# Half of the first norm's modulation tiles as the stationary operand of TensorE, and eleven tile buffers

## The chip, the core and the metric

One core of a Trainium2 chip runs the whole kernel. The metric is the device time of one execution in microseconds (us), as the median of three runs. Beside it stands one profiled execution, in which every instruction is recorded.

## The reference, cut to what matters

The program is a block with a state-space scan, a gating unit and a mixture of experts, followed by a two-layer attention block. The change touches only the first thing that it computes from its conditioning vectors, the shift and scale of the first norm:

```
mod_l = silu(c)     @ ada_w + ada_b      # c, c_ctx: 1024 values; ada_w: 1024 x 6144
mod_c = silu(c_ctx) @ ada_w + ada_b
sh1, sc1 = first two blocks of 1024 of mod_l (and of mod_c)
xm_c = rmsnorm(ctx, norm1_w) * (1 + sc1_c) + sh1_c     # 256 x 1024
xm_l = rmsnorm(x,   norm1_w) * (1 + sc1_l) + sh1_l     # 512 x 1024
```

All later work takes `xm_l` and `xm_c` as input. So two vectors (latent and context) are multiplied with the first 2048 columns of `ada_w`, which is a matrix of 1024 rows: 8 MB in float32.

## The kernel before, in words

`main` (L750) runs `setup`, loads parameters, and calls `norm_x` (L223), `ada01` (L176), `mod_x` (L252) and `scan` (L314). The kernel is written against a framework that records instructions, tracks their dependences and then writes a fixed order for each engine: earlier lines of the program have priority, and where an instruction isn't ready, a later one that is goes ahead of it. So the order on an engine is fixed at build time, and at run time each engine takes its own list in turn and waits where an input is not there.

`norm_x` loads six 128x1024 blocks of tokens (`xin`, L233), squares and sums them on ScalarE (L235), makes the inverse root on VectorE (`rsqrt`, L151), scales the blocks (L241) and turns them with 48 TensorE transposes of 128x128 into `aux` banks of PSUM (L248), from where ScalarE and VectorE copy them to `xr` (L249). There are four `aux` banks and four `mm` banks (L90, L93).

`ada01` makes the shift and scale. The 16 tiles `araw` are loaded by SyncE's queue in the order j = 0, 1 (the 1024 columns of shift, then of scale) and k = 0 to 7 (the 128-row blocks of `ada_w`); there are eight buffers for them (L202, L203). Float32 products are made of the engine's rounded float32 format by splitting an operand in a high and a low part. Each tile passes `split` (L101): ScalarE writes the high part `whi` (L106), VectorE the low part `wlo` (L107). The two vectors are split as well and stand as four columns `st[:, k]`, which are the stationary operand; the tile's parts move, 512 columns at a time. That is four matmuls for a tile (L207 twice, L208 twice), each with 4 stationary columns and 512 moving ones, summed over k in two `mm` banks of 4 rows. The result is copied by ScalarE to `ada_res` (L210). Then 16 small matmuls (L213, eight for each j) with `ada_res` as the stationary operand and a selection matrix `sel` of two columns as the moving one add high and low and turn rows to columns: 128 features on the partitions, two columns for each block, all in one `aux` bank `pm`. These are plain float32 matmuls, and each is issued as two pairs of a weight load and a matmul. VectorE makes `shf` and `scl` of them (L218 to L220).

`mod_x` applies them, with ScalarE (L265), VectorE (L266, L267) and GpSimd (L267), and what it writes is the input of `dt_proj` (L346) and of the projections (L272), whose products are L115 to L117.

SyncE's queue carries all loads. It has at most eight loads under way: load n waits until load n-8 has landed. In program order behind the tiles stand six loads of the scan: `dsk` (L325), `w_dt` (L98), `dtb` and `alog` (L364), and two weight tiles `w_xbc` (L98). As the ninth `araw` tile has to wait for a buffer, the order before puts these six between the eighth and the ninth tile.

Elsewhere the same form of matmul as in L213 is found in the router of the experts (L853): a whole float32 tile of 128x128 as the stationary operand and 16 moving columns.

```
201            for k in range(8):
202                raw = e1.tile([128, 1024], F32, name="araw", tag="araw", bufs=8)
203                nc.sync.dma_start(raw, self.a["ada"][k * 128:(k + 1) * 128, j * 1024:(j + 1) * 1024])
204                wh, wl = self.split(raw, 1024)
```

Of the kernel before, what the change touches and what calls it, by code (L numbers as in the profile page):

```python
# [8 lines left out]
F32 = mybir.dt.float32  # L9
# [28 lines left out]
class Net:  # L38
# [51 lines left out]
    def mm(self):  # L90
        return self.ps.tile([128, 512], F32, name="mm", tag="mm", bufs=4)
# [84 lines left out]
    def ada01(self):  # L176

        nc, sm = self.nc, self.c1
        ct = sm.tile([128, 16], F32, name="ct")
        th = sm.tile([128, 16], F32, name="cth")  # L180
        nc.scalar.activation(th, self.PA[:, 0:16], AF.Tanh, scale=0.5)
        nc.vector.tensor_scalar(ct, self.PA[:, 0:16], 0.5, None, op0=OP.mult)
        self.cs = cs = self.c1.tile([128, 16], F32, name="cs")
        nc.vector.scalar_tensor_tensor(cs, th, 1.0, ct, op0=OP.add, op1=OP.mult)
        st = self.c1.tile([128, 8, 4], F32R, name="cst")
        nc.vector.tensor_copy(st[:, :, 0], cs[:, 0:8])
        nc.vector.tensor_copy(st[:, :, 2], cs[:, 8:16])
        nc.vector.tensor_tensor(st[:, :, 1], cs[:, 0:8], st[:, :, 0].bitcast(F32), OP.subtract)
        nc.vector.tensor_tensor(st[:, :, 3], cs[:, 8:16], st[:, :, 2].bitcast(F32), OP.subtract)
        jp = sm.tile([4, 2], I32, name="jp4")  # L190
        nc.gpsimd.iota(jp, pattern=[[-2, 2]], base=0, channel_multiplier=1)
        s1 = sm.tile([4, 2], F32, name="s1")
        sel = sm.tile([4, 2], F32, name="sel")
        nc.vector.tensor_scalar(s1, jp, 0.0, None, op0=OP.is_ge)
        nc.vector.tensor_scalar(sel, jp, 1.0, None, op0=OP.is_le)
        nc.vector.tensor_tensor(sel, sel, s1, OP.mult)
        e1 = self.e1
        res = e1.tile([4, 2048], F32, name="ada_res")
        for j in range(2):
            pp = [self.mm(), self.mm()]  # L200
            for k in range(8):
                raw = e1.tile([128, 1024], F32, name="araw", tag="araw", bufs=8)  # L202
                nc.sync.dma_start(raw, self.a["ada"][k * 128:(k + 1) * 128, j * 1024:(j + 1) * 1024])  # L203
                wh, wl = self.split(raw, 1024)
                for q in range(2):
                    c = slice(q * 512, (q + 1) * 512)
                    nc.tensor.matmul(pp[q][:4], st[:, k], wh[:, c], start=k == 0, stop=False)  # L207
                    nc.tensor.matmul(pp[q][:4], st[:, k], wl[:, c], start=False, stop=k == 7)  # L208
            for q in range(2):
                nc.scalar.copy(res[:, j * 1024 + q * 512:j * 1024 + (q + 1) * 512], pp[q][:4])  # L210
        pm = self.aux()
        for b in range(16):
            nc.tensor.matmul(pm[:, 2 * b:2 * b + 2], res[:, b * 128:(b + 1) * 128], sel, start=True, stop=True)  # L213
        pv = pm[:, :32].rearrange("p (b s) -> p s b", s=2)
        self.scl = self.c1.tile([128, 2, 8], F32, name="scl")
        self.shf = self.c1.tile([128, 2, 8], F32, name="shf")
        for s in range(2):
            nc.vector.tensor_tensor(self.shf[:, s], pv[:, s, 0:8], self.PA[:, 24:32], OP.add)  # L218
            nc.vector.scalar_tensor_tensor(self.scl[:, s], pv[:, s, 8:16], 1.0, self.PA[:, 32:40], op0=OP.add, op1=OP.add)
            nc.vector.tensor_tensor(self.scl[:, s], self.scl[:, s], self.PA[:, 16:24], OP.mult)  # L220
        e1.release()
# [1844 lines left out]
```

## Time and profile before

| What | Value |
|---|---|
| Median of 3 runs | 3218.07 us (3213.55 to 3218.97) |
| Profiled execution, its own time | 3218.56 us |
| Its span | 3216.8 us (1.76 us of its time lie around the span) |
| TensorE busy (matmul) | 3053.1 us, 95% |
| VectorE, ScalarE, GpSimd busy | 70%, 50%, 12% |
| Mean granted clock of TensorE | 0.977 of full speed |
| First instruction of `mod_x` | 47.16 us after the span's start |

The profile gives busy time for each engine, a record for each instruction with its start and duration, what ended the idle time ahead of it, and the clock that TensorE was granted. A matmul's end is modelled, so the pace of a row of matmuls is read from their starts. PE stands for TensorE's matmuls, PEld for its weight loads, DVE for VectorE, ACT for ScalarE, POOL for GpSimd, SPq for SyncE's queue of loads.

### The profile page before, as it was taken

The numbers are of one execution on the slowest core, as the hardware profiler recorded it, in microseconds if no ns is written. First come the engines' busy times: TensorE is split into PE (matmuls) and PEld (weight loads), VectorE is DVE, ScalarE is ACT, GpSimd is POOL, SyncE is SP. The second block draws the span as 40 slices with busy tenths as digits, with TensorE's granted clock in tenths as the row PEclk, the third lists the DMA queues.
The fourth block names the chain that finished last, engine by engine and source line by source line (L and its number), as shares of the span: only waits on it lengthen the run. The fifth ranks groups of instructions, "written<-read, shape, count | busy, mean of one in ns | idle before, by whom it ended". The sixth has DMA issues, their size and how long they took to land. (4 is left out here: it accounts for less than half of the span.)

```text
span 3216.8 us, 43492 instructions
## 1 busy us (share of the span) xinstructions
PE 3053.1 (95%) x16242; PEld 2484.7 (77%) x16242; DVE 2255.6 (70%) x3786; ACT 1592.5 (50%) x2715; POOL 378.3 (12%) x295
## 2 busy tenths in 40 slices
PE   7999899969999999699999999999999999999998
PEld 4887677756656556578787789988888777799986
DVE  7778764468988878767575588863776655688844
ACT  6545432228767667356353435552464444445531
POOL 1454200032211111200011000000000010000000
PEclk9999999979999999899999999999999999999999
DMA  5112434549999997311215333332312224323322
GB/s 193 53 46 73 144 122 147 197 179 393 371 345 348 347 335 271 105 59 60 86 47 173 99 118 99 106 98 93 105 53 74 79 99 140 110 92 109 106 92 79
DMA packets 140781, 470.06 MB, mean 146 GB/s; under 512 B 16268, under 2 KB 20364, under 8 KB 140568
## 3 DMA queue, kind: packets, MB, share of 16 engines
q1 hardware_dynamic: 139416, 463.08, 41.4%
q0 software_dynamic: 1152, 4.19, 0.4%
q8 instruction: 127, 2.08, 0.3%
q14 instruction: 86, 0.70, 0.1%
HBM read 456.71 MB, written 10.50 MB: 145 GB/s over the span
## 5 line engine op out<-in xcount | busy, mean ns | idle before, releaser
L107 DVE TENSOR_TENSOR wlo<-raw,whi 128x1024 fp32r<-128x1024 f32 (+4 forms) x340 | 379.3, 1118 | 310.8 <-ACT whi L106 309.5
L106 ACT CAST whi<-raw 128x1024 fp32r<-128x1024 f32 (+4 forms) x340 | 317.7, 936 | 412.1 <-PE mm L116 155.4
L115 PE MATMUL mm<-xTh,whi 128*128 128x512 f32 (+2 forms) x880 | 344.1, 391 | 4.8 <-ACT P L1240 2.6
L116 PE MATMUL mm<-xTh,wlo 128*128 128x512 f32 (+3 forms) x880 | 340.7, 388 | 0.0
L117 PE MATMUL mm<-xTl,whi 128*128 128x512 f32 (+2 forms) x880 | 338.8, 386 | 1.1 <-DVE xTl L267 0.6
L115 PE MATMUL mm<-whi,xTh 128*128 128x512 f32 (+1 forms) x536 | 206.8, 388 | 6.1 <-DVE zt L562 3.5
L117 PE MATMUL mm<-wlo,xTh 128*128 128x512 f32 (+1 forms) x536 | 204.5, 387 | 3.8 <-DVE wlo L107 3.8
L116 PE MATMUL mm<-whi,xTl 128*128 128x512 f32 (+1 forms) x536 | 206.9, 386 | 0.0
L115 PEld LDWEIGHTS mm<-xTh,whi 128*128 128x128 f32 (+1 forms) x880 | 165.5, 188 | 45.5 <-ACT P L1240 4.2
L117 PEld LDWEIGHTS mm<-xTl,whi 128*128 128x128 f32 (+1 forms) x880 | 165.3, 188 | 38.1 <-DVE xTl L267 2.2
L116 PEld LDWEIGHTS mm<-xTh,wlo 128*128 128x128 f32 (+1 forms) x880 | 165.6, 188 | 34.3 <-issue 1.2
L1013 PE MATMUL mm<-wlo,XS 128*128 128x512 f32 x336 | 113.6, 412 | 15.7 <-DVE wlo L952 13.2
L115 PEld LDWEIGHTS mm<-whi,xTh 128*128 128x128 f32 x536 | 101.4, 189 | 27.5 <-DVE zt L562 4.3
L1404 POOL TENSOR_TENSOR ql<-q,qh 128x512 fp32r<-128x512 f32 x16 | 20.7, 1292 | 862.6 <-ACT qh L1403 862.6
L117 PEld LDWEIGHTS mm<-wlo,xTh 128*128 128x128 f32 x536 | 101.3, 189 | 23.6 <-DVE wlo L107 4.2
L116 PEld LDWEIGHTS mm<-whi,xTl 128*128 128x128 f32 x536 | 101.4, 189 | 19.5
L952 DVE TENSOR_TENSOR wlo<-mraw,whi 128x1024 fp32r<-128x1024 f32 x82 | 107.0, 1328 | 12.8 <-ACT whi L950 12.2
L1012 PE MATMUL mm<-whi,XS 128*128 128x512 f32 x336 | 111.5, 408 | 2.5 <-ACT whi L950 2.5
L950 ACT CAST whi<-mraw 128x1024 fp32r<-128x1024 f32 x96 | 97.6, 1048 | 26.3 <-PE mm L1012 22.9
L1240 ACT ACTIVATE P<-mm,smv 128x512 f32<-128x512 f32 x128 | 88.2, 691 | 31.7 <-DVE P L1528 16.0
L115 PE MATMUL mm<-whi,hh 128*128 128x512 f32 x248 | 94.9, 398 | 8.1 <-ACT hh L1854 8.0
L107 DVE TENSOR_TENSOR flo<-fs,fhi 128x1024 fp32r<-128x1024 f32 x80 | 97.7, 1221 | 5.7 <-ACT fhi L106 4.6
(827 smaller groups left out, 8664.2 us busy)
## 6 DMA issues: line engine op xcount, KB each, us to landing
raw<-w_f SPq DMA_DIRECT2D x92, 512.0 KB
raw<-w_gate SPq DMA_DIRECT2D x68, 512.0 KB
mraw<-w_gate SPq DMA_DIRECT2D x52, 512.0 KB
mraw<-w_down SPq DMA_DIRECT2D x49, 512.0 KB
araw<-ada SPq DMA_DIRECT2D x48, 512.0 KB
mraw<-w_up SPq DMA_DIRECT2D x43, 512.0 KB
rawu<-w_f SPq DMA_DIRECT2D x40, 512.0 KB
PT<-w_up SPq DMA_DIRECT2D x30, 512.0 KB
```

Source lines behind the costliest of these rows:

```text
L106: nc.scalar.copy(hi[:, :n], raw[:, :n])
L107: nc.vector.tensor_tensor(lo[:, :n], raw[:, :n], hi[:, :n].bitcast(F32), OP.subtract)
L115: mm(out, ah, bh, start=first, stop=False)
L116: mm(out, al, bh, start=False, stop=False)
L117: mm(out, ah, bl, start=False, stop=last)
L950: nc.scalar.copy(hi, raw)
L952: eng.tensor_tensor(lo, raw, hi.bitcast(F32), OP.subtract)
L1012: nc.tensor.matmul(pp[q], X[:, k], wh[:, c], start=k == 0, stop=False)
L1013: nc.tensor.matmul(pp[q], X[:, k], wl[:, c], start=False, stop=k == 7)
L1240: nc.scalar.activation(P, s, AF.Exp, bias=v[:, 8 + i:9 + i], accum_out=v[:, 16 + i:17 + i])
L1404: nc.gpsimd.tensor_tensor(ql, q, qh.bitcast(F32), OP.subtract)
```

## The change

Of the eight tiles of each j, four still pass `split` and the moving matmuls (k = 0, 2, 4, 6 for j = 0 and k = 0, 1, 3, 4 for j = 1). The other four are used as they land: each of their eight 128x128 blocks is the stationary operand of a plain float32 matmul with the two silu columns of that k as the moving operand. These sum directly in `pm`, where the L213 matmuls of the four split tiles are added too; `pm` is begun by the first whole-tile matmul and never cleared again. The eight L213 matmuls of each j follow the copies of that j. The tiles have eleven buffers in place of eight.

```
-        for j in range(2):
+        c2 = cs.rearrange("p (s k) -> p k s", s=2)
+        mm = nc.tensor.matmul
+        pm = self.aux()
+        out = lambda b: pm[:, 2 * b:2 * b + 2]
+        begun = False
+        for j, rows in enumerate(((0, 2, 4, 6), (0, 1, 3, 4))):
             pp = [self.mm(), self.mm()]
             for k in range(8):
-                raw = e1.tile([128, 1024], F32, name="araw", tag="araw", bufs=8)
+                raw = e1.tile([128, 1024], F32, name="araw", tag="araw", bufs=11)
                 nc.sync.dma_start(raw, self.a["ada"][k * 128:(k + 1) * 128, j * 1024:(j + 1) * 1024])
+                if k not in rows:
+                    for b in range(8):
+                        mm(out(8 * j + b), raw[:, b * 128:(b + 1) * 128], c2[:, k], start=not begun, stop=True, skip_group_check=begun)
+                        begun = True
+                    continue
                 wh, wl = self.split(raw, 1024)
                 for q in range(2):
                     c = slice(q * 512, (q + 1) * 512)
-                    nc.tensor.matmul(pp[q][:4], st[:, k], wh[:, c], start=k == 0, stop=False)
-                    nc.tensor.matmul(pp[q][:4], st[:, k], wl[:, c], start=False, stop=k == 7)
+                    mm(pp[q][:4], st[:, k], wh[:, c], start=k == rows[0], stop=False)
+                    mm(pp[q][:4], st[:, k], wl[:, c], start=False, stop=k == rows[-1])
             for q in range(2):
                 nc.scalar.copy(res[:, j * 1024 + q * 512:j * 1024 + (q + 1) * 512], pp[q][:4])
-        pm = self.aux()
-        for b in range(16):
-            nc.tensor.matmul(pm[:, 2 * b:2 * b + 2], res[:, b * 128:(b + 1) * 128], sel, start=True, stop=True)
+            for b in range(8 * j, 8 * j + 8):
+                mm(out(b), res[:, b * 128:(b + 1) * 128], sel, start=False, stop=True, skip_group_check=True)
```

## Rows read from the trace of the kernel before

**Rows 1.** The page: busy time of TensorE, and its busy tenths in 40 slices.
```profile
PE 3053.1 (95%) x16242; PEld 2484.7 (77%) x16242; DVE 2255.6 (70%) x3786; ACT 1592.5 (50%) x2715; POOL 378.3 (12%) x295
...
PE   7999899969999999699999999999999999999998
```
**Rows 2.** Timeline 39 to 48: start us, us, engine, line, operation, tiles, count [idle before].
```profile
39.71 1.05 ACT L106 CAST whi<-araw 128x1024 fp32r<-128x1024 f32 x1 [0.20 <-DMA araw<-ada]
...
42.30 0.62 PE L208 MATMUL mm<-wlo,cst 128*4 128x512 f32 x2
...
43.28 1.05 ACT L210 COPY ada_res<-mm 4x512 f32<-4x512 f32 x2
...
43.91 2.72 PE L213 MATMUL aux<-sel,ada_res 4*128 4x2 f32 x16 [0.99 <-ACT ada_res L210]
46.66 0.17 DVE L218 TENSOR_TENSOR shf<-aux,PA 128x8 f32<-128x8 f32 x1 [1.81 <-PE aux L213]
...
47.16 9.69 ACT L265 ACTIVATE xTh<-xr,shf,scl 128x512 fp32r<-128x512 f32 x16 [2.83 <-DVE scl L220]
```
**Rows 3.** Timeline of PE alone, 14 to 37.
```profile
14.43 1.01 PE L207 MATMUL mm<-whi,cst 128*4 128x512 f32 x2 [10.88 <-ACT whi L106]
...
16.68 1.05 PE L207 MATMUL mm<-whi,cst 128*4 128x512 f32 x2
17.54 1.05 PE L208 MATMUL mm<-wlo,cst 128*4 128x512 f32 x2
...
20.10 1.03 PE L207 MATMUL mm<-whi,cst 128*4 128x512 f32 x2
...
23.82 0.62 PE L208 MATMUL mm<-wlo,cst 128*4 128x512 f32 x2
24.27 0.63 PE L207 MATMUL mm<-whi,cst 128*4 128x512 f32 x2
...
27.76 1.31 PE L248 MATMUL aux<-ident,xin 128*128 128x128 f32 x10 [0.36 <-ACT xr L249]
28.82 0.70 PE L208 MATMUL mm<-wlo,cst 128*4 128x512 f32 x2
...
33.72 1.94 PE L213 MATMUL aux<-sel,ada_res 4*128 4x2 f32 x16
35.59 0.63 PE L208 MATMUL mm<-wlo,cst 128*4 128x512 f32 x2
36.06 0.62 PE L207 MATMUL mm<-whi,cst 128*4 128x512 f32 x2
```
**Rows 4.** One tile's instructions (araw): count, duration ns min/median/max, first and last start.
```profile
L106 ACT CAST whi<-araw x16: 1030/1046/1056, 13.3 to 39.7; 128x1024 fp32r<-128x1024 f32 x16
L107 DVE TENSOR_TENSOR wlo<-araw,whi x16: 1214/1219/1227, 14.6 to 41.0; 128x1024 fp32r<-128x1024 f32 x16
```
**Rows 5.** Timeline of SyncE's queue: the araw loads before and behind the other six.
```profile
4.56 7.82 SPq L203 DMA_DIRECT2D araw<-ada  x8
...
21.05 8.60 SPq L203 DMA_DIRECT2D araw<-ada  x8
```
**Rows 6.** Timeline of PE: the router's whole tiles as stationary operand, at either clock.
```profile
663.09 3.44 PE L853 MATMUL aux<-wrp,xT 128*128 128x16 f32 x16
...
683.19 1.85 PE L853 MATMUL aux<-wrp,xT 128*128 128x16 f32 x16
```
**Rows 7.** Windows: busy of PE, PEld, DVE, ACT, POOL (counts), granted clock, DMA share, GB/s.
```profile
662.69:666.10 3.41, 3.18 (x16) 3.21 (x17) 0.09 (x1) 0.93 (x4) 0.44 (x3) 0.50 0.37 154
...
683.17:686.58 3.41, 3.31 (x30) 3.19 (x28) 2.66 (x11) 1.71 (x7) 0.00 (x0) 1.00 1.00 390
686.58:689.99 3.41, 1.94 (x9) 1.63 (x9) 2.72 (x11) 0.54 (x4) 0.55 (x3) 0.50 1.02 401
...
1324.87:1328.28 3.41, 3.41 (x17) 3.12 (x16) 3.34 (x13) 1.58 (x3) 0.00 (x0) 0.50 0.64 263
1328.28:1331.69 3.41, 3.41 (x24) 3.41 (x24) 3.21 (x12) 0.76 (x2) 0.00 (x0) 1.00 0.12 47
```
**Rows 8.** Timeline of PEld: weight loads of transposes at the lower clock.
```profile
1326.62 1.66 PEld L1141 LDWEIGHTS aux<-ident,h 128*128 128x128 f32 x8
```

## The prediction

> **What bounds the kernel now.** The page comes first: TensorE is busy in 95% of the span and in nine tenths or more of nearly every slice, with one low digit at the very start [rows 1]. Time is therefore lost or won here where the chain that feeds TensorE's first long work is late. The timeline of the first 48 us shows that chain. `mod_x` starts on ScalarE at 47.16, released by `scl`; VectorE had waited for the last of the L213 matmuls, which ended at about 46.6 [rows 2]. All later work takes what `mod_x` writes, so I count a shift of this point as a shift of the end. I found no later stretch that could swallow it: the loads of the experts' weights, the busiest stretch of the DMA engines, are issued as buffers come free and move along.
>
> What makes the point 46.6? The last tile lands at about 39.5: ScalarE's last cast starts at 39.71, after an idle 0.20 us that a load ended [rows 2]. Then come cast, subtraction, two matmuls (at 42.30), two copies (from 43.28) and eight L213 matmuls in 16 pairs (from 43.91) [rows 2]. So the tail behind the last landing is 46.6 - 39.5 = 7.1 us, and the landings set the rest.
>
> The timeline of PE alone shows how near TensorE is to setting it too. Two matmuls of 512 columns take 17.54 - 16.68 = 0.86 us early and 24.27 - 23.82 = 0.45 to 36.06 - 35.59 = 0.47 us later [rows 3]. That is TensorE at the lower and the upper of its two clock levels (1.2 and 2.4 GHz): it starts at the lower one and changes between the rows at 20.10 and 23.82, after it has been fed without a gap. (The clock column of the windows has its first record only there, so before it I go by this pace.) I take 21. At the upper level a tile costs four matmuls, 2 x 0.47 = 0.94 us; a transpose (28.82 - 27.76) / 10 = 0.106; a pair of L213 (35.59 - 33.72) / 16 = 0.117 [rows 3]. TensorE's work from 14.43 on is then 16 x 0.94 + 48 x 0.106 + 32 x 0.117 = 15.0 + 5.1 + 3.7 = 23.8 us. The lower level until 21 wastes half of 6.6 us, 3.3. The second L213 group takes 2.72 instead of 1.94 [rows 2, 3], 0.8 more. Together 27.9 us of the 32.2 from 14.43 to 46.6; only 4.3 us are waits. This is the number that matters: TensorE has little room there.
>
> **The change, part by part.** *Removed:* eight casts of 1.046 us on ScalarE and eight subtractions of 1.219 on VectorE [rows 4], 8.4 and 9.8 us. They lie beside the loads, except for the last tile's, which stand in the tail. Also 32 moving matmuls, eight tiles x 0.94 = 7.5 us of TensorE.
>
> *Added:* eight tiles x eight matmuls. The router has the same form, a whole 128x128 float32 tile as the stationary operand and few moving columns; eight matmuls are 16 pairs and take 1.85 us at the upper level and 3.44 at the lower [rows 6]. The moving columns are 16 there and 2 here; the L213 pairs with 2 have the same pace (0.117 against 1.85 / 16 = 0.116), so the weight loads set it. A whole tile thus costs TensorE twice what a split tile does: 1.85 against 0.94 at the upper level, 3.44 against 2 x 0.86 = 1.72 at the lower. Over eight tiles that is +7.3 us or +13.8.
>
> *Moved:* the order of the loads. With eleven buffers the ninth to eleventh tile can go ahead of the six other loads, which stand now between the two groups of eight [rows 5]. The bytes ahead of the last tile stay the same, so I leave its landing at 39.5. The bounds: if TensorE is late with a whole tile, its buffer is late and so is the load that waits for it, up to 2 us; if all 16 tiles went ahead of the other six loads, it would land earlier by at most the gap between the two groups of issues, 21.05 - (4.56 + 7.82) = 8.7 us [rows 5]. I take 0, the nearer end, as five tiles still have to wait for buffers and the six other loads do not. No issue is added. *The one bank `pm`* is held from the first whole tile on, so the transposes go round with three banks, not four. They run beside casts and loads; I cost it at nothing, and at 1 us if TensorE waits for a copy in each of a few rounds.
>
> *The waits that go:* TensorE no longer waits for `wlo` of eight tiles, and the last tile needs no cast and no subtraction. Behind its landing stand 1.85 us of pairs, and the 16 L213 pairs of j = 1 can be done earlier or beside. *What is late next:* TensorE's own list. Its work at the upper level is 8 x 0.94 + 8 x 1.85 + 5.1 + 3.7 = 31.1 us. It can't start before the second tile has landed, at about 14.4, as now. The time at the lower level costs half of itself. Whole tiles in between will not bring the clock up sooner than the unbroken stream of 512 columns did; I take 9 us (to 23.5) where it was 6.6: 4.5 us wasted. The last three tiles of j = 1 are all whole, 5.6 us of weight loads in a row; the clock falls about there, as it did in the last L213 group, and I keep the same 0.8. Sum: 14.4 + 31.1 + 4.5 + 0.8 = 50.8, with no waits left, because TensorE is behind its inputs. Against 46.6 that is +4.2 us. The profiled execution would take 3218.56 + 4.2 = 3222.8; the median of the runs is 0.5 lower, so **3222**.
>
> **A row and a rule on the clock.** In the stretch 683.17 to 686.58 TensorE does almost nothing but such pairs, weight loads busy 3.19 of 3.41 us; the clock granted is 1.00, and in the next stretch it is 0.50 [rows 7]. From 662.69 to 666.10 it does nothing else either, 3.18 us busy, at 0.50, and the clock isn't raised for the next pairs of that row: 16 take all the 3.44 us [rows 6, 7]. So a TensorE full of weight loads with few moving columns is treated as idle. The Trainium skill, in TensorE: Matmul & The Clock Gate, section "Why this matters for your kernels", puts drops of the clock inside a kernel down to gaps in which TensorE is idle. By that rule TensorE, which has no gaps here, would keep the upper level once it has it: the sum would be without the 0.8, +3.4 us and 3221. The rows disagree with the rule as far as this form goes, and they speak against the change. The other way round, a stretch full of transposes and a few matmuls (1324.87 to 1328.28, busy 3.41 of 3.41) ran at 0.50 and the next is granted 1.00 [rows 7]; so transposes do lift it.
>
> **The rivals.** *The lower clock stays (slower).* Place: from 14.4 on. Whole tiles stand between the split ones and the transposes in TensorE's list, and each is 3.44 us of what counts as idle. If no stretch is dense enough to lift the clock before the last tile, the work is 8 x 1.72 + 8 x 3.44 + 48 x 0.21 + 32 x 0.215 = 13.8 + 27.5 + 10.1 + 6.9 = 58.3 us (0.21 = 1.66 / 8 from [rows 8], 0.215 = 3.44 / 16), ending at 72.7: +26, **3244**. It decides from the point where the first lift would come; if it comes at 35 instead of 23.5, half of the 11.5 more is lost, +10, 3228; the same follows if the clock falls amid the last whole tiles for all of them. For it: the rows above. Against it: the transposes, which are issued in rows of ten or so now [rows 3] and stand among split tiles.
>
> *The tail goes and TensorE keeps up (faster).* If the clock were up early and the work of TensorE fitted between the landings, the end would be 39.5 + 1.85 + 0.2 = 41.6 in place of 46.6: -5, **3213**; with the tiles ahead of the other loads up to 8.7 more, 3204. For it: 18 us are taken off ScalarE and VectorE, and waits for `wlo` go. Against it: the 31.1 us need 14.4 + 31.1 = 45.5 even with no time at the lower level, which is -1.1 at best. It can only be if the pairs are quicker than in the router, or if later work gains by another order.
>
> *It is swallowed.* The end shifts, but `mod_x` or TensorE's first products have slack behind them, or whole tiles are put last in the lists: 3218, no change. Little speaks for it: TensorE is at nine tenths from the second slice on [rows 1].
>
> **How the numbers follow.** What a measurement of this kernel can tell from no change is about 0.2%, 6.4 us. TensorE behind, the clock lifted by the transposes: 0.42, from 3219 to 3224, within. The lower level for much of the stretch or for all of it, 3225 to 3244: 0.45, slower. The faster case: 0.09, of which 0.06 passes 6.4 us. Swallowed: 0.04. So faster 0.06, same 0.42 + 0.04 + 0.03 = 0.49, slower 0.45. The likeliest is the first, 3222, with its own range 3219 to 3224; the range that holds 8 in 10 takes in all of the slower case and of the faster one only what lies near: 3214 to 3244.
>
> **What would show it.** Right: TensorE without idle time from 15 to the start of `shf`; whole tiles with 16 pairs in 1.85 or 3.44 us; `shf` at about 51, VectorE and ScalarE idle in 25 to 48; the rest of the trace the same, shifted. The clock rival: two matmuls of 512 columns still 0.86 apart at 30 and later, `shf` past 60. Wrong: `shf` before 46, or pairs well below 0.11 us; or a time that differs while `shf` doesn't move, which would put the cause behind 48.

## The result, and the profile after

The changed kernel took 3237.26 us (median of five runs, 3235.27 to 3240.94); the kernel before, beside it, 3218.07. The ratio is 1.0062 [1.0051, 1.0073]: slower by 19.2 us. That is inside the range and on the side of the slower rival; the likeliest case, 3222, did not come. The profiled execution took 3240.94 us for a span of 3239.2; it is the slowest of the five.

The page of the changed kernel, busy time and TensorE's tenths and clock in 40 slices (answers to [rows 1]):

```profile
PE 3077.3 (95%) x16338; PEld 2511.7 (78%) x16338; DVE 2241.5 (69%) x3778; ACT 1583.0 (49%) x2707; POOL 376.9 (12%) x295
...
PE   8999899979989999699999999999999999999998
...
PEclk7999899989999999899999999999999999999999
```

The same row of clock in the kernel before:

```profile
PEclk9999999979999999899999999999999999999999
```

TensorE has 24.2 us more to do by its busy time (3077.3 against 3053.1) and the others have less. The first slice is busier than before (8 against 7 in its row), and the clock granted there is 7 tenths, where the page of before has 9. So the loss to look for is in the first slice (80 us), and it isn't idle time. The timeline of PE there, start, us, line, operation, tiles, count (answers to [rows 3]; lines from L213 on are 9 higher than before: L211 is the whole tiles' matmul, L217 and L218 the split tiles', L222 the former L213, L257 the transposes, L227 `shf`):

```profile
16.90 1.02 PE L217 MATMUL mm<-whi,cst 128*4 128x512 f32 x2
17.71 0.67 PE L257 MATMUL aux<-ident,xin 128*128 128x128 f32 x2
...
22.37 0.93 PE L218 MATMUL mm<-wlo,cst 128*4 128x512 f32 x2
23.14 0.63 PE L217 MATMUL mm<-whi,cst 128*4 128x512 f32 x2
23.61 0.38 PE L257 MATMUL aux<-ident,xin 128*128 128x128 f32 x2
...
29.46 1.05 PE L257 MATMUL aux<-ident,xin 128*128 128x128 f32 x8
30.35 11.14 PE L211 MATMUL aux<-cs,araw 128*128 128x2 f32 x64
41.42 3.57 PE L222 MATMUL aux<-sel,ada_res 4*128 4x2 f32 x16
44.92 3.58 PE L211 MATMUL aux<-cs,araw 128*128 128x2 f32 x16
48.36 0.59 PE L217 MATMUL mm<-whi,cst 128*4 128x512 f32 x1
48.75 0.63 PE L218 MATMUL mm<-wlo,cst 128*4 128x512 f32 x1
...
51.73 10.23 PE L211 MATMUL aux<-cs,araw 128*128 128x2 f32 x48
61.90 3.57 PE L222 MATMUL aux<-sel,ada_res 4*128 4x2 f32 x16
```

Two things stand here that the prediction didn't have. First, no whole tile starts before the last transpose: all four of j = 0 follow in one group of 64 pairs at 30.35. Second, the pairs are slow nearly throughout: 16 take 44.92 - 41.42 = 3.50 us, 0.219 each, and the eight split matmuls at 48.36 start 0.43 apart. That is the lower level. The windows of the same kernel say where it begins (us, then busy time of PE, PEld, DVE, ACT, POOL, then the clock granted):

```profile
23.00:30.00 7.00, 7.00 (x47) 4.67 (x45) 5.38 (x10) 5.46 (x10) 0.00 (x0) 1.00 0.81 307
30.00:40.00 10.00, 10.00 (x63) 10.00 (x61) 3.51 (x5) 3.06 (x5) 0.00 (x0) 0.66 0.79 308
40.00:50.00 10.00, 10.00 (x44) 8.79 (x44) 0.00 (x0) 0.16 (x1) 0.00 (x0) 0.50 0.00 0
50.00:60.00 10.00, 10.00 (x45) 8.97 (x43) 2.45 (x2) 2.88 (x4) 0.00 (x0) 0.50 0.31 107
```

0.66 from 30 to 40 is 1.00 until about 33.2 and 0.50 after it. So the level falls about 3 us after the pairs begin, with TensorE busy all the time, and it is still 0.50 when the last pairs are done (0.50 from 60 to 66 as well). VectorE and ScalarE are idle from 40 to 50 and mostly idle beside it. What sets the end (answers to [rows 2]):

```profile
65.51 0.17 DVE L227 TENSOR_TENSOR shf<-aux,PA 128x8 f32<-128x8 f32 x1 [11.61 <-PE aux L222]
...
66.00 2.22 ACT L274 ACTIVATE xTh<-xr,shf,scl 128x512 fp32r<-128x512 f32 x3 [12.88 <-DVE scl L229]
```

`shf` starts at 65.51 in place of 46.66, 65.51 - 46.66 = 18.85 us later, and the medians differ by 19.2.

### The profile page after: what moved, and what is told of

The parts are those of the page before. It is cut to its first block, busy times and chain, and to the rows that moved or that the text cites. A ratio compares the mean times of both kernels' runs of the same rounds, so it can differ in the third digit from the quotient of the medians.

```text
span 3239.2 us, 43653 instructions
## 1 busy us (share of the span) xinstructions
PE 3077.3 (95%) x16338; PEld 2511.7 (78%) x16338; DVE 2241.5 (69%) x3778; ACT 1583.0 (49%) x2707; POOL 376.9 (12%) x295
## 5 line engine op out<-in xcount | busy, mean ns | idle before, releaser
L115 PE MATMUL mm<-xTh,whi 128*128 128x512 f32 (+3 forms) x880 | 345.0, 392 | 6.9 <-DVE cc L300 3.0
L116 PE MATMUL mm<-xTh,wlo 128*128 128x512 f32 (+2 forms) x880 | 341.0, 388 | 0.0
L117 PE MATMUL mm<-xTl,whi 128*128 128x512 f32 (+3 forms) x880 | 339.5, 387 | 0.2 <-DVE xTl L276 0.2
L1022 PE MATMUL mm<-wlo,XS 128*128 128x512 f32 x336 | 115.0, 415 | 14.4 <-DVE wlo L961 9.9
```

What stands on the lines that cost most here:

```text
L115: mm(out, ah, bh, start=first, stop=False)
L116: mm(out, al, bh, start=False, stop=False)
L117: mm(out, ah, bl, start=False, stop=last)
L1022: nc.tensor.matmul(pp[q], X[:, k], wl[:, c], start=False, stop=k == 7)
```

## The experiments

The theory after this was: TensorE's list in the first 66 us is the whole loss, made of more work (about 4 us) and of the lower clock while pairs run in a row (about 15). The rivals: the loads' order or the eleven buffers; the bank `pm`, whose late turn puts the whole tiles behind the transposes; the pairs being slow for another reason than the clock; slack or another loss further back. The moment of `shf` is the measure of the front; the time also holds what comes behind.

**Only the eleven buffers.**

```
-raw = e1.tile([128, 1024], F32, name="araw", tag="araw", bufs=8)
+raw = e1.tile([128, 1024], F32, name="araw", tag="araw", bufs=11)
```

> The kernel before with eleven tile buffers and nothing else. Theory (TensorE's pairs and its clock make the loss): the last tile still lands behind the six other loads, so shf starts at 46 to 47.5 as before and the time is that of before within 3 us. Rival (the moved loads make part of the loss): shf later than 48, 3221 us or more.

Measured: 3217.3 us, ratio 0.9997 [0.9988, 1.0006], `shf` at 44.38, which is sooner than either side expected. The buffers and the loads' order are not the loss.

**Another bank for `pm`.**

```
-pm = self.aux()
+pm = self.mm()
```

> The changed kernel with pm in an mm bank, so that the whole tiles don't stand behind the transposes. Theory (the loss comes from all whole tiles standing in a row, where the clock falls): they now run from 15 us on among split tiles and transposes; if that stretch still lifts the clock, shf starts at 50 to 56, 3222 to 3228 us. Rival (the price is that of the pairs at the lower clock wherever they stand, and early ones keep the clock from being lifted at all): shf at 65 to 73, 3236 to 3244 us.

Measured: 3237.3 us, ratio 1.005 [1.0036, 1.0063], `shf` at 60.13. Some rows of its timeline of PE:

```profile
14.96 3.41 PE L211 MATMUL mm<-cs,araw 128*128 128x2 f32 x16
20.10 2.13 PE L211 MATMUL mm<-cs,araw 128*128 128x2 f32 x10
...
28.03 1.27 PE L211 MATMUL mm<-cs,araw 128*128 128x2 f32 x6
...
33.98 0.50 PE L211 MATMUL mm<-cs,araw 128*128 128x2 f32 x4
...
45.97 1.84 PE L211 MATMUL mm<-cs,araw 128*128 128x2 f32 x16
...
50.54 6.06 PE L211 MATMUL mm<-cs,araw 128*128 128x2 f32 x38
56.53 3.57 PE L222 MATMUL mm<-sel,ada_res 4*128 4x2 f32 x16
```

So it was the choice of the bank that put the whole tiles behind the transposes: now they start at 14.96. But these early pairs run at the lower level (16 in 3.41 us), and six still take 1.27 us at 28.03; the clock is lifted between there and the four in 0.50 us at 33.98, where it had been lifted near 23. It falls twice later (the granted clock is 0.70 from 40 to 50; then the 38 pairs at 50.54 take 6.06 us, the last 16 take 3.57). `shf` comes 5.4 us sooner than in the changed kernel, not the 10 to 15 of the theory, and the time doesn't follow: it is that of the rival. `shf` is 13.5 us later than before and the median 19.5; the order of work behind wasn't held here, and what the 6 us are stays open. The bank sets the order; either order loses to the clock.

**Fillers between the pairs.** One matmul of 512 columns on constant data behind every second whole-tile matmul (32 in all), then behind every one (64). `issue_after` keeps a filler behind its matmul in TensorE's list; the lines that make `fill` are left out here:

```
+pf = self.mm()
 ...
 i = mm(out(8 * j + b), raw[:, b * 128:(b + 1) * 128], c2[:, k], ...)
+if b % 2:   # "if True:" in the run with 64
+    with self.tc.issue_after(i.ins if hasattr(i, "ins") else i):
+        mm(pf[:4], st[:, k], fill, start=True, stop=True)
```

> The changed kernel with one more matmul of 512 moving columns behind every second matmul of a whole tile (four for a tile, 32 in all, their result is not used). Theory (a row of weight loads with two moving columns lets the clock fall): the added columns keep the clock at the upper level, a whole tile takes 1.85 + 4 x 0.235 = 2.8 us in place of 3.44, shf starts at about 58.5 in place of 65.5, 3230 us, faster with more work. Rival (pairs cost what they cost, the clock is not the cause): 32 x 0.235 to 0.43 us are added, shf at 73 to 79, 3245 to 3251 us.

> The changed kernel, with one filler matmul of 512 columns behind each of the 64 whole-tile matmuls, twice as many as in the run with four a tile. Theory (the clock is what costs): this is dense enough to keep the upper level, so the pairs stay at 0.116 us and a filler at 0.235; 64 x 0.47 = 30.1 us for the whole tiles, shf at 66 to 70, 3237 to 3242 us, not slower than with 32 fillers although there is more work. Rival (fillers of any number don't hold the level, or the slow pairs aren't the clock's doing): 64 x 0.86 = 55 us, shf at 88 to 96, 3258 to 3268.

Measured with 32: 3243.56 us, ratio 1.007 [1.0056, 1.0083], `shf` at 74.04. The theory's numbers failed and the rival's `shf` came, though not for the rival's reason: the level still fell (the whole tiles start at 29.43; from 34.54 on a filler starts 0.38 us ahead of the next pairs instead of 0.24, and the granted clock is 0.50 from 40 to 74). With 64: 3242.89 us, ratio 1.007 [1.0056, 1.0085], `shf` at **62.08**, 4 us sooner than the theory had it; the time is 0.9 us above its range. The timeline of PE of the run with 64 (here L215 is the whole tile, L218 the filler, L229 the former L213, L224 and L225 the split tiles):

```profile
29.44 0.39 PE L218 MATMUL mm<-fill,cst 128*4 128x512 f32 x1
29.67 0.28 PE L215 MATMUL aux<-cs,araw 128*128 128x2 f32 x2
29.80 0.39 PE L218 MATMUL mm<-fill,cst 128*4 128x512 f32 x1
...
41.12 1.94 PE L229 MATMUL aux<-sel,ada_res 4*128 4x2 f32 x16
42.99 0.39 PE L224 MATMUL mm<-whi,cst 128*4 128x512 f32 x1
...
44.31 0.63 PE L225 MATMUL mm<-wlo,cst 128*4 128x512 f32 x1
...
47.62 0.40 PE L218 MATMUL mm<-fill,cst 128*4 128x512 f32 x1
47.85 0.28 PE L215 MATMUL aux<-cs,araw 128*128 128x2 f32 x2
```

and its windows:

```profile
30.00:40.00 10.00, 10.00 (x84) 8.91 (x82) 1.22 (x1) 1.28 (x2) 0.00 (x0) 1.00 0.57 221
40.00:50.00 10.00, 10.00 (x61) 7.14 (x60) 1.56 (x2) 1.45 (x2) 0.00 (x0) 0.83 0.16 54
50.00:62.00 12.00, 12.00 (x94) 10.12 (x92) 2.36 (x2) 2.95 (x4) 0.00 (x0) 1.00 0.28 88
```

This shows that the clock is what costs. TensorE issues 64 more matmuls of 512 columns than in the changed kernel and is done 3.4 us sooner, because the clock is granted at 1.00 nearly throughout; in the stretch of the whole tiles it is low only for some 3.4 us, behind the first group of 16 pairs without fillers (41.12). A whole-tile matmul and its filler together repeat every 0.37 us there, less than the 2 x 0.219 = 0.44 that its two pairs alone take in the changed kernel, so the pairs aren't slow by themselves. The time didn't follow: `shf` is 15.4 us later than before, the median 25. In the profiled execution (3238.39, the runs go from 3234.15 to 3244.63) 4 us are added behind. The order of work behind wasn't held in this run (see the last four), but the loads behind the front stand in the order of the kernel before, so a moved order is not the likely reason; what the 9.5 us are stays open.

**Half of the change.** Whole tiles in j = 0 alone, then in j = 1 alone, both with eleven buffers. (In these runs and the next two, `pm` is begun by whichever matmul comes first; those lines are left out.)

```
-for j, rows in enumerate(((0, 2, 4, 6), (0, 1, 3, 4))):
+for j, rows in enumerate(((0, 2, 4, 6), (0, 1, 2, 3, 4, 5, 6, 7))):   # j = 0 alone
+for j, rows in enumerate(((0, 1, 2, 3, 4, 5, 6, 7), (0, 1, 3, 4))):   # j = 1 alone
```

> The first half of the change alone: whole tiles only in j = 0 (k = 1, 3, 5, 7), j = 1 all split, eleven buffers. Theory (order and clock together): the four whole tiles again come in a row behind the transposes from about 30, the clock falls some 3 us later, whole tiles and sel group take 11 + 3.6 us, then 32 matmuls of 512 columns, which lift the clock again on their way: shf at 55 to 60, 3226 to 3232 us. Rival (only the late start of the whole tiles counts, the clock does not fall): 30.4 + 7.4 + 1.9 + 7.5 + 1.9 = shf at 49, 3219 to 3222.

> The second half of the change alone: whole tiles only in j = 1 (k = 2, 5, 6, 7), j = 0 all split, eleven buffers. The whole tiles don't keep the transposes or a bank waiting here, as they come last anyway. Theory (the clock): the sel group, the four whole tiles and the last sel group are 96 pairs almost in a row from about 36; the clock falls inside them at about 40 and the rest goes at 0.215: shf at 52 to 58, 3224 to 3231 us. Rival (the late start behind the bank was the cost in the changed kernel, a run of pairs is nothing by itself): all at 0.116, shf at 46 to 49, 3217 to 3221, as before.

Measured: j = 0 alone 3227.15 us, ratio 1.0025 [1.0015, 1.0035], `shf` at 56.08, as the theory has it. Its timeline of PE shows the same group of 64 pairs and then how the level comes back: the split matmuls start 0.43 apart up to 49.71, and from 50.45 on two start 0.47 after the two before.

```profile
30.71 11.33 PE L211 MATMUL aux<-cs,araw 128*128 128x2 f32 x64
41.98 3.57 PE L222 MATMUL aux<-sel,ada_res 4*128 4x2 f32 x16
...
49.28 0.63 PE L218 MATMUL mm<-wlo,cst 128*4 128x512 f32 x1
49.71 0.91 PE L217 MATMUL mm<-whi,cst 128*4 128x512 f32 x2
50.45 0.63 PE L218 MATMUL mm<-wlo,cst 128*4 128x512 f32 x2
50.92 0.62 PE L217 MATMUL mm<-whi,cst 128*4 128x512 f32 x2
...
54.10 1.94 PE L222 MATMUL aux<-sel,ada_res 4*128 4x2 f32 x16 [1.17 <-ACT ada_res L220]
```

j = 1 alone: `shf` at 54.40, as the theory has it, but 3215.18 us, ratio 0.9993 [0.9984, 1.0002]: no slower than before. Here the theory's time failed, with the theory's trace; it is even under the rival's 3217 to 3221. Somewhere behind, 10 us had been won. Pairing the matmuls of this trace with those of the kernel before, counted from the end, puts this in the experts' stage: the lag is 9.7 us at 1000, 6.1 at 1100 and -1.9 at 1200.

**One or two tiles whole.** The kernel before, with only the last tile or the last two of j = 1 whole, eight buffers:

```
-for j, rows in enumerate(((0, 2, 4, 6), (0, 1, 3, 4))):
+for j, rows in enumerate(((0, 1, 2, 3, 4, 5, 6, 7), (0, 1, 2, 3, 4, 5, 6))):   # last one
+for j, rows in enumerate(((0, 1, 2, 3, 4, 5, 6, 7), (0, 1, 2, 3, 4, 5))):      # last two
```

> The kernel before with one whole tile, the very last (j = 1, k = 7), eight buffers. Theory (one whole tile costs 16 pairs, and only the row of them lets the clock fall): behind the last landing at 39.6 stand 1.9 to 3.4 us of pairs and no cast, subtraction or copy; shf at 43 to 45, 2 to 4 us faster than before, 3214 to 3216 us. Rival (a whole tile costs more than it saves wherever it stands): shf at 47 or later, 3218 us or more.

> The kernel before with only the last two tiles whole (j = 1, k = 6 and 7), eight buffers. Theory (a short run of pairs fits before the clock falls, and behind the last landing stands no cast): shf at 43 to 46, 3211 to 3216 us. Rival (each whole tile costs TensorE more than it saves, and the gain of the one last tile was only its cast): shf at 46 to 49, 3217 to 3221.

Measured: the last one 3212.13 us, ratio 0.9983 [0.9974, 0.9992], `shf` at 44.61; the last two 3215.46, ratio 0.9988 [0.9979, 0.9997], `shf` at 45.98, time and `shf` as the theory of that run has them. The gain of the first, 5.6 us, is more than the 2 us of `shf` and more than was expected: again something behind.

**The order behind held.** The built programs of these kernels showed what it is. The framework writes the order of every engine from a plan of the whole program, and a change of the first stage shifted that plan: behind `mod_x`, loads and splits of the experts' weights stand in another order than in the kernel before. With only the buffers changed nothing differs behind the front. So the last four runs hold the order from `mod_x` on to a given one, by edges that set the order of issue and no wait (`ISSUE_ORDER`, left out here, is the list of places):

```
+def keep_order(self):
+    D, C, R = mybir.DependencyInfo, mybir.DependencyClass, mybir.DependencyReason
+    L = list(self.nc.cur_bb.bb.instructions)
+    for d in json.loads(zlib.decompress(base64.b85decode(ISSUE_ORDER))).values():
+        at, prev = 0, None
+        for x in d:
+            at += x
+            i = L[len(L) - 1 - at]
+            if prev is not None:
+                self.tc.add_manual_dep(i, prev.name, D(C.NoSync, R.DATA), reason="order")
+            prev = i
```

> The changed kernel, with the order of every engine's instructions from mod_x on held to that of the kernel before. The planner that writes the orders sees the whole program, so the edit also changed some orders in the experts' stage (the first loads that differ stand near the 70th of SyncE's list). Theory (the shift of shf, 18.9 us, is the whole cost, and the other order behind is worth little here): 3234 to 3240 us. Rival (the other order behind hid part of the cost, as it seems to in the run with whole tiles in j = 1 alone, where shf came 7.7 us later and the time was 2.7 us shorter): 3242 to 3249.

> Whole tiles in j = 1 alone, eleven buffers, with the order from mod_x on held to that of the kernel before. Theory (a later shf costs what it is later; the gain came from the planner's other order in the experts' stage): shf at 54 again, 3224 to 3228 us. Rival (some stage behind has slack and swallows the shift): 3213 to 3218.

> Only the last tile whole, eight buffers, with the order from mod_x on held to that of the kernel before. Theory (the earlier shf gains its own 2 us, the rest of the 5.6 us was the other order): 3215 to 3217 us. Rival (all of it comes from the front): 3211 to 3213.

> The kernel before, nothing changed in the first norm, with the order from mod_x on held to that of the kernel with the last tile whole. Theory (the order by itself is worth a few us): 3211 to 3216 us, shf at 46.7 as before. Rival (the order is worth nothing): 3217 to 3219.

Measured:

| Kernel | `shf` at | us | ratio to before |
|---|---|---|---|
| change, order of before | 63.01 | 3236.69 | 1.0064 [1.005, 1.0078] |
| j = 1 alone, order of before | 54.87 | 3227.22 | 1.003 [1.0018, 1.0042] |
| last tile whole, order of before | 45.73 | 3215.85 | 0.9999 [0.999, 1.0008] |
| kernel before, order of "last tile whole" | 45.23 | 3211.41 | 0.9984 [0.9975, 0.9993] |

All four times came as the theory has them; in the last, `shf` came at 45.23 and not at 46.7. The kernel before wasn't run with its own order held, but the pair of kernels stands in for it: with either front, the order of before gives the time of before (3217.19, 3215.85) and the other order 4 to 6 us less (3211.41, 3212.13), so holding an order costs little by itself. With the order held, j = 1 alone costs 10 us where `shf` is 8.2 us later (beside the 46.66 of before); its other order had hidden that. And the kernel before, with nothing changed in the first norm, is 5.8 us faster with the other order: the gain of the last tile whole was that, not the tile. The groups of PE in the stretch 1100 to 1200 of that last kernel show a stretch where it is won; paired as above, the matmuls lie 0.4 us behind at 1100 and 8.9 ahead at 1200 (line, operation, count | busy, mean ns | idle before, releasers; lines 13 higher than before):

```profile
L1026 PE MATMUL mm<-wlo,XS 128*128 128x512 f32 x60 | 19.5, 406 | 2.1 <-DVE wlo L965 2.1
L1025 PE MATMUL mm<-whi,XS 128*128 128x512 f32 x60 | 19.2, 403 | 0.9 <-ACT whi L963 0.9
```

The same two groups in the kernel before:

```profile
L1013 PE MATMUL mm<-wlo,XS 128*128 128x512 f32 x60 | 20.3, 417 | 5.7 <-DVE wlo L952 4.4 <-POOL wlo L952 1.3
L1012 PE MATMUL mm<-whi,XS 128*128 128x512 f32 x60 | 19.6, 408 | 1.6 <-ACT whi L950 1.6
```

In these two groups TensorE waits 3.0 us for split weights in place of 7.3, and in all it is busy for 94.71 of the 100 us in place of 91.02. Which of the moved entries does it wasn't tried.

The first run of the table shows one thing more. TensorE's list in the front is that of the changed kernel, matmul for matmul, yet `shf` is 2.5 us sooner. Behind the same eight split matmuls the level rose for a while, and the 48 pairs take 7.14 us where they took 10.23:

```profile
52.33 7.14 PE L211 MATMUL aux<-cs,araw 128*128 128x2 f32 x48
...
49.00:52.00 3.00, 3.00 (x9) 0.88 (x10) 0.48 (x1) 1.32 (x2) 0.00 (x0) 0.50 0.00 0
52.00:56.00 4.00, 4.00 (x35) 3.91 (x33) 1.97 (x2) 1.72 (x3) 0.00 (x0) 0.93 0.55 154
56.00:63.00 7.00, 6.97 (x33) 6.87 (x32) 0.00 (x0) 0.00 (x0) 0.00 (x0) 0.50 0.18 66
```

So what the lower level costs differs between executions of one list, and a single `shf` is good to some 2.5 us; the 1 to 2 us by which it comes sooner with one or two tiles whole are not clear of that.

## Why the prediction was right or wrong

- **What bounds the kernel: right for a later `shf`.** It is a later end, with the order behind unchanged: 63.01 - 46.66 = 16.35 us later against a median 19.5 longer (change), 8.2 against 10.0 (j = 1 alone), 9.4 against 9.2 (j = 0 alone, where little differs behind). The single `shf` is of one execution, and it moves by itself: in the run with the kernel before's own front it was 45.23, 1.4 us from the 46.66 of before. For a sooner `shf` it isn't shown: with the eleven buffers alone it came 2.3 us sooner and the median is 0.5 less; paired as above, the matmuls are 3.2 us ahead at 1000 and 0.6 at 1100, so a stage behind did swallow a lead there.
- **The pace of the pairs and the sum of the work: right.** A pair takes 0.116 at the upper and 0.212 to 0.219 us at the lower level, as the router's [rows 6].
- **The lower level at the start, 9 us: right.** The level rises near 22.9 (from 23.14 on two matmuls start 0.47 apart); forecast 23.5. It was right for another reason than given, which is luck: no whole tile stood in that stretch at all. That transposes lift the level is borne out: from 17.71 to 22.37 TensorE did nothing but transposes, 16 of them.
- **The end, "I keep the same 0.8": this is the step that failed.** It took the fall of the clock amid the last whole tiles for a thing as short as in the kernel before [rows 2]. The level fell at about 33.2 and stayed down for the rest: some 39 of the 64 pairs and the groups of 16, 16, 48 and 16, 135 pairs in all, at 0.219 in place of 0.116, and eight split matmuls at 0.43 in place of 0.235, which is 13.9 + 1.6, about 15 us where 0.8 stood. Without them `shf` would come at about 50, which is the likeliest case's 50.8.
- **Why it failed: the bank `pm` at "nothing to 1 us".** I had the whole tiles spread among split tiles and transposes. With `pm` in an `aux` bank they came only behind the last transpose, so nearly all the pairs stand in one piece, with just eight split matmuls among them. The run with `pm` in an `mm` bank shows that the bank sets this order. But it also shows that the spread that I had assumed would have cost the clock as well, later lifted and lifted less: 60.13.
- **The rival "the lower clock stays": right in mechanism, wrong in place.** I put it from 14.4 on, where it gives 72.7, or at +10 us by a late first lift or a fall amid the last whole tiles. It was an early lift and a fall amid the first ones, 65.51; its sign, `shf` past 60, came. The range held because this rival was in it, not by the sum of the likeliest case. The chance of 0.45 for it was about fair, but [rows 7] had shown both halves of it, the fall from 1.00 to 0.50 in a TensorE full of such pairs and no lift by them; with 160 pairs in the list that spoke for more.
- **Costed at nothing and right:** the loads' order and the eleven buffers (ratio 0.9997), the casts and subtractions that went (not tried alone; TensorE has no gap from 30.35 on in which it could wait for one).
- **Left without a price in the prediction:** that the plan behind moves too (it says only "if later work gains by another order", in the faster rival). For this change it is worth little: 3237.26 with its own order, 3236.69 with that of before.

On the rule: the Trainium skill, in TensorE: Matmul & The Clock Gate, section "Why this matters for your kernels", puts drops inside a kernel down to gaps with TensorE idle. From 30.35 to the last pair TensorE shows no gap here, with weight loads busy for 10.00 of 10.00 us from 30 to 40, and the granted clock falls to 0.50 all the same. The measurement decides: the rule doesn't cover what TensorE did here, weight loads for two moving columns each.

## What to carry to other kernels

A matmul with a large stationary operand and a few moving columns costs its weight loads and, in a row, the clock of what stands behind it, here until the first products behind `shf` (from 71 on matmuls of 512 columns start 0.23 apart again): keep them few in a row, and look at what the clock does to the work behind them (one tile at the end cost nothing here, eight in the middle and at the end cost 19 us). Look at which buffer or bank the first of them waits for, since that decides what they stand next to. Where a planner orders the whole program, an edit of one stage can move another; before a difference of some us is put down to the edit, hold the order elsewhere and measure again.

## What the hardware showed that I had not expected

- The clock fell with TensorE busy without a gap (30.35 on), with four fillers of 512 columns for a whole tile as well, and not amid the tiles with eight.
- A weight load goes beside a filler: a whole-tile matmul and its filler repeat every (40.80 - 29.44) / 31 = 0.366 us (the 32 fillers of j = 0), where two pairs and 512 columns one after the other would be 2 x 0.116 + 0.235 = 0.467.
- More work was quicker: 64 added matmuls of 512 columns brought `shf` from 65.51 to 62.08.
- One list of TensorE, in two executions, had its level raised once or twice, and `shf` at 65.51 or 63.01.
- The order in which loads and splits stand, alone, was worth 5.8 us of 3217.
